# Sixty-four tokens return from the dense experts to the gathered ones, and sixteen expert products stand beside the gate table

## The chip, the core and the metric

One core of a Trainium2 chip runs the whole program. Its engines work side by side, each in the order in which its instructions stand: PE (TensorE, matrix products), DVE (VectorE), ACT (ScalarE), POOL (GpSimd, which here also issues the indirect gathers) and SP (SyncE, which issues the plain DMAs). Sixteen DMA engines move the data of both kinds of DMA. The metric is the device time of one execution in microseconds, the median of several runs.

## The reference

One layer of a hybrid decoder for a prompt of 1024 tokens and a sample group of 32 tokens (8 sequences of 4). The last part of it is where the time goes: each token picks 8 x 16 of 16384 experts by a product-key search, and sums their outputs.

```python
proj = x @ W_in                      # [z | x_ssd | B | C | dt | q | k | v]
m    = [SSD(...) ; DilatedWindowAttention(q, k, v)] @ W_out
h    = LayerNorm1(ALPHA * x + m)
# PEER(h), per token: 8 heads, 16 experts of 16384 each
s1, s2 = q[..., :128] @ keys_1, q[..., 128:] @ keys_2      # 128 keys each
e, g   = the 16 best of the pairs of the 16 best keys, softmax of their scores
hid    = gelu(u_tab[e] . h)
out    = LayerNorm2(ALPHA * h + sum((g * hid) * v_tab[e]))
```

All arrays are float32. The kernel splits an operand into a high and a low part and adds three products (high x high, low x high, high x low), so that a 1024-deep product of 128 outputs takes 24 matrix instructions for each piece of columns.

## The kernel before

**Two ways to the same expert sum.** Of the prompt tokens some are gathered: for each of its 128 picks a token fetches the expert's row of `u` (4 KB), DVE multiplies and sums it (L1871), and after the gelu it fetches the row of `v` and DVE adds it in (L1876). One instruction fetches one pick for 128 tokens, a `row` of 512 KB (L1845, on POOL's queue). The other tokens are dense: every expert is computed for every one of them, in 128 products with `ut` (128 experts each, "hidden") and 128 with `vd` (128 outputs each over 8 x 128 experts, "output"), and a table of gates that is zero nearly everywhere weighs the hidden values. The table is built on the chip (`gates`), stored to DRAM (`gd`) and read back chunk by chunk.

**Stages.** Part 0 handles the first 512 prompt tokens and the 32 sample tokens, part 1 the other 512 prompt tokens. Each part runs `first` (projections and attention), `second` (convolutions, the scan over chunks, and z), `third` (output projection and norm) and `route` (the key search). `dense` then does the expert products for TE tokens in two pieces of columns, `TPC`. Before, EXTRA = 64 prompt tokens of part 0 are taken out of the gathered group and put beside part 1's 512 and the 32 samples: TE = 608 in pieces of 320 and 288 columns, and 448 gathered tokens. These make 3 full groups of 128 tokens (256 rows each), and one of 64, whose 128 picks are packed as two halves of 64 partitions (`half_e`, `half_g`) and so take 128 rows: 896 rows.

**What sets the order.** The program is written out by hand. A product (`step`, `proj`, `product`) hands its instructions to PE in a number of equal shares, and after each share a tick runs every waiting generator ("lane") by its rate. `GATHER` sets how many rows the gather lane (`gathers`, `pumping`) takes for each projection of part 1: 2.5 in `first`, 3.2 in `second`, 3 in `third`, none in `route`, and 0.2 for each tick beside the table. In `dense` the rate spreads what is left evenly over the ticks. `LOOK` = 5 rows are fetched ahead into `ROWS` = 6 buffers, so the fetch of row k+5 waits until DVE has used row k-1.

**The table and what stands beside it.** `gates` takes four tokens at a time (a group): DVE compares (L1624, `oo`), POOL multiplies (L1626), PE multiplies four times (L1633), ACT copies out (L1643). 608 tokens make 152 groups. The list `EARLY` gives the ticks of the expert products that run between the groups: six of the first chunk's eight hidden products, in 8 to 40 shares. The last two of that chunk follow when the table is done.

**The dense loop.** For each chunk c of 1024 experts there are eight hidden products (PE writes PSUM, ACT gelu L1689, DVE weighs L1693, ACT and DVE split into `ah`, `al`), then eight output products that DVE adds up (L1717). Each product's 512 KB of weights is loaded in two halves (`wraw`), split by ACT (`whi`, L366) and by DVE or POOL (`wlo`, L367, by the list LO5 one in seven on DVE), two products ahead of its use. During a chunk's output products the next chunk's table is read (`g<-gd`). L447 and L1767 are the matrix instructions; in the first pass over the weights, part 0, split weights are stored to DRAM (`ws`), and part 1 loads these.

## Time and profile before

| | |
|---|---|
| median of 3 runs | 3749.65 us (3748.82 to 3754.33) |
| the profiled execution | 3745.24 us |
| span of its instructions | 3743.3 us |
| PE / DVE / ACT / POOL busy | 3461.4 / 2600.5 / 1205.4 / 2231.0 us |
| moved by DMA | 994.91 MB, of it 469.82 MB by POOL's queue |
| mean granted clock of PE | 0.965 of full speed |

The span runs from the first to the last instruction of the core, so the execution is 1.9 us longer than it. Busy shares are means over stages with different limits; what follows reads stages one at a time. A DMA share is the mean busy share of the 16 DMA engines in a stretch, and it can read a few hundredths above 1.

### The profile page before, as it was taken

The page shows a single profiled execution, that of the slowest core. Times are in us where ns is not written, and L with a number is a line of the kernel's source. Part 1 is how long each engine was busy: PE and PEld are TensorE (multiplying, and loading weights), DVE is VectorE, ACT ScalarE, POOL GpSimd, SP SyncE. Part 2 cuts the span into 40 slices and gives each one's busy share as a digit, 9 for nine tenths or more (in the row PEclk, how much of TensorE's full clock was granted, in tenths as well). Part 3 has the DMA queues.
Part 4 walks back from the last instruction along what each step waited for, and adds up shares of the span by engine and source line. Part 5 has one row for each costly group of instructions (what it writes and reads, how often), then busy time and mean ns, then how long its engine had stood idle before and what let it go on. Part 6 is the DMA issues. An engine that isn't in the chain of part 4 may idle for free.

```text
span 3743.3 us, 61910 instructions
## 1 busy us (share of the span) xinstructions
PE 3461.4 (92%) x22691; PEld 3132.8 (84%) x22691; DVE 2600.5 (69%) x5394; ACT 1205.4 (32%) x2195; POOL 2231.0 (60%) x2138
## 2 busy tenths in 40 slices
PE   7999999989799888896778999999999999999998
PEld 6757778988567666675777999999999999999997
DVE  2325654379668987589998867677767667777775
ACT  3422224252343233123565222222232222223223
POOL 3303555333444676313887877777778777777774
PEclk9999899999899999997889999999999999999999
DMA  7565447996557669742557999999999999999994
GB/s 248 192 207 185 144 149 241 371 343 214 163 168 293 235 217 337 304 141 72 202 204 267 342 328 339 336 322 314 320 326 356 330 329 335 321 315 321 333 330 138
DMA packets 452624, 994.91 MB, mean 266 GB/s; under 512 B 47712, under 2 KB 158688, under 8 KB 449376
## 3 DMA queue, kind: packets, MB, share of 16 engines
q1 hardware_dynamic: 323296, 521.14, 41.1%
q0 software_dynamic: 129024, 469.82, 34.6%
q8 instruction: 179, 2.93, 0.3%
q14 instruction: 125, 1.02, 0.1%
HBM read 845.18 MB, written 174.34 MB: 272 GB/s over the span
## 4 chain that ended last, share of the span: by engine, by line
PE 53%; DVE 16%; DMA 5%; POOL 5%; issue 4%; ACT 2%; SPq 0%; POOLq 0%; DVEq 0%; ACTq 0%
PE P L447 42%; PE P L1767 5%; DVE oo L1624 2%; DMA wlo<-ws 2%; DVE cv L751 2%; DVE row L1871 1%; PE P L712 1%; POOL row L1845 1%; DVE mr L1363 1%; PE P L689 1%; POOL oo L1626 1%; DVE keys L1367 1%; DVE keys L1361 1%; PE P L1633 1%; POOL eq L1564 1%
## 5 line engine op out<-in xcount | busy, mean ns | idle before, releaser
L367 POOL TENSOR_TENSOR wlo<-wraw,whi 128x512 fp32r<-128x512 f32 x524 | 678.5, 1300 | 495.6 <-ACT whi L366 438.5
L366 ACT ACTIVATE whi<-wraw 128x512 fp32r<-128x512 f32 (+1 forms) x668 | 406.1, 625 | 1305.7 <-PE P L447 563.7
L447 PE MATMUL P<-hh,whi 128*128 128x320 f32 (+3 forms) x2648 | 656.2, 313 | 13.4 <-DMA whi<-ws 5.7
L447 PE MATMUL P<-hl,whi 128*128 128x320 f32 (+3 forms) x2648 | 653.4, 311 | 3.2 <-POOL hl L1318 2.9
L447 PE MATMUL P<-hh,wlo 128*128 128x320 f32 (+3 forms) x2648 | 647.4, 310 | 7.6 <-DMA wlo<-ws 3.9
L1876 DVE SCALAR_TENSOR_TENSOR P<-row,hid,P 128x1024 f32<-128x1024 f32 x448 | 575.8, 1285 | 40.3 <-DMA row<-in_v,ecol 23.9
L1871 DVE SCALAR_TENSOR_TENSOR row<-row,P 128x1024 f32<-128x1024 f32 x403 | 478.8, 1214 | 66.1 <-DMA row<-in_u,ecol 29.6
L1845 POOL DMA_INDIRECT row<-in_u,ecol x384 | 386.9, 1008 | 191.6 <-DVE row L1871 100.9
L447 PEld LDWEIGHTS P<-hh,whi 128*128 128x128 f32 x2648 | 445.5, 191 | 24.9 <-DMA whi<-ws 7.0
L447 PEld LDWEIGHTS P<-hh,wlo 128*128 128x128 f32 x2648 | 443.7, 190 | 17.7 <-DMA wlo<-ws 5.9
L447 PE MATMUL P<-xh,whi 128*128 128x272 f32 (+4 forms) x1288 | 431.2, 345 | 27.0 <-ACT xh L366 15.0
L447 PEld LDWEIGHTS P<-hl,whi 128*128 128x128 f32 x2648 | 444.9, 191 | 12.6 <-POOL hl L1318 4.2
L1845 POOL DMA_INDIRECT row<-in_v,ecol x384 | 375.9, 979 | 118.4 <-DVE P L1876 47.1
L447 PE MATMUL P<-xl,whi 128*128 128x272 f32 (+4 forms) x1288 | 418.8, 335 | 7.4 <-POOL xl L367 6.8
L447 PE MATMUL P<-xh,wlo 128*128 128x272 f32 (+4 forms) x1288 | 417.4, 334 | 3.2 <-DMA wlo<-ws 3.2
L447 PE MATMUL P<-ah,wlo 128*128 128x320 f32 (+1 forms) x1536 | 341.8, 302 | 3.6 <-POOL wlo L367 3.6
L447 PE MATMUL P<-ah,whi 128*128 128x320 f32 (+1 forms) x1536 | 342.8, 302 | 0.0
L447 PE MATMUL P<-al,whi 128*128 128x320 f32 (+1 forms) x1536 | 341.5, 301 | 0.0
L447 PEld LDWEIGHTS P<-xh,whi 128*128 128x128 f32 (+1 forms) x1288 | 246.6, 195 | 57.5 <-ACT xh L366 16.6
L367 DVE TENSOR_TENSOR wlo<-wraw,whi 128x512 fp32r<-128x512 f32 (+1 forms) x144 | 133.6, 928 | 229.8 <-ACT whi L366 210.4
L447 PEld LDWEIGHTS P<-xl,whi 128*128 128x128 f32 (+1 forms) x1288 | 246.5, 195 | 33.9 <-POOL xl L367 8.7
L447 PEld LDWEIGHTS P<-xh,wlo 128*128 128x128 f32 (+1 forms) x1288 | 245.8, 195 | 29.4 <-DMA wlo<-ws 5.0
(386 smaller groups left out, 6110.7 us busy)
## 6 DMA issues: line engine op xcount, KB each, us to landing
wraw<-in_ut SPq DMA_DIRECT2D x256, 256.0 KB, 5.4
wraw<-in_vd SPq DMA_DIRECT2D x256, 256.0 KB, 5.0
ws<-whi SPq DMA_DIRECT2D x152, 256.0 KB, 5.1
ws<-wlo SPq DMA_DIRECT2D x152, 256.0 KB, 5.0
whi<-ws SPq DMA_DIRECT2D x152, 256.0 KB, 5.2
wlo<-ws SPq DMA_DIRECT2D x152, 256.0 KB, 5.5
gd<-gst SPq DMA_DIRECT2D x19, 2048.0 KB, 7.5
g<-gd SPq DMA_DIRECT2D x90, 320.0 KB, 10.9
```

The costliest lines, as they stand in the source:

```text
L366: nc.scalar.activation(hi, src, AF.Copy)
L367: (eng or nc.vector).tensor_tensor(lo, src, hi.bitcast(F32), op=ALU.subtract)
L447: nc.tensor.matmul(outs[i], w[a][:, k, :m], x[b][k][:, s:s + n], start=first and st, stop=last and sp)
L689: nc.tensor.matmul(sc[:, a:b], qz[:, hh, qt * 128:(qt + 1) * 128], kk[:, a:b], start=True, stop=True)
L712: nc.tensor.matmul(pv[row, :128], vv[:, k, row], pT[:, k, :], start=k == 0, stop=k == nt - 1)
L751: nc.vector.scalar_tensor_tensor(cv[:, 3:n], xr[:, k:k + m], cw[:, k:k + 1], cv[:, 3:n], op0=ALU.mult, op1=ALU.add)
L1361: nc.vector.max_index(idx[:, 0:8], vals[:, 0:8], src)
L1624: nc.vector.tensor_tensor(oo, iota.unsqueeze(1).unsqueeze(1).to_broadcast([128, 2, 4, 128]), eT[:, 0:2, t0:t0 + 4].unsqueeze(3).to_broadca ...
L1767: nc.tensor.matmul(outs[i][j], self.ws[q0 + i][wi][:, e, :], x[xi][e][:, s:s + m], start=e == p == 0, stop=e == last and p == 2)
L1845: nc.gpsimd.indirect_dma_start(out=rows[k], out_offset=None, in_=t["uv"[tab]], in_offset=bass.IndirectOffsetOnAxis(ap=tables(gi)[0][:, s:s ...
L1871: nc.vector.scalar_tensor_tensor(r, r, 1.0, at, op0=ALU.mult, op1=ALU.mult, accum_out=hid[:, s:s + 1])
L1876: nc.vector.scalar_tensor_tensor(at, r, hid[:, s:s + 1], at, op0=ALU.mult, op1=ALU.add)
```

## The change

The gathered group takes back the 64 tokens: 512 gathered tokens, 1024 rows, and TE = 544 dense tokens in pieces of 288 and 256 columns. The half-packed tables and their sum at the end go. The table has 136 groups. Beside it stand sixteen hidden products instead of six (`BEFORE`, `EARLY`): the eight of chunk 0, and the first two of each of chunks 1 to 4. The results of these last eight wait in DRAM (`ed`) until their chunk's turn, when `recall` loads them and `recalled` weighs and splits them. The dense loop (`STEPS`) has 240 products instead of 248. The rows of the gathers are drawn faster in part 1. The sample tokens' groups come first in the table, and its lane waits there until the key search is done.

```diff
-EXTRA = 64
-TG = TD - EXTRA
-NX = EXTRA + NS
-TE = PD + NX
+TE = PD + NS
...
-GATHER = [2.5, 3.2, 3, 0.0, 0.2]
+GATHER, GATHERT = [[0, 0, 0, 0], [4, 4.2, 3.5, 0.0]], 0.2
...
-EQ, OBUFS, EARLY = 4, 4, [8, 16, 24, 30, 34, 40]
+EQ, OBUFS, EARLY = 4, 4, [8] + [9] * 13 + [4] * 2
+AHEAD = {1: 2, 2: 2, 3: 2, 4: 2}
+BEFORE = [(0, 0, k) for k in range(8)] + [(c, 0, k) for c in AHEAD for k in range(AHEAD[c])]
+STEPS = [s for s in ((c, half, k) for c in range(NE // 8) for half in range(2) for k in range(8)) if s not in BEFORE]
...
+        self.ed = {(c, k): dpool.tile([128, TE], F32, name=f"ed{c}{k}") for c in AHEAD for k in range(AHEAD[c])}
...
-        work = [(NS, PD + EXTRA, 0), (EXTRA, PD, 128 - EXTRA)] + [(m, s, 0) for s, m in tiles]
-        given = 2
+        work = [(NS, PD)] + list((m, s) for s, m in tiles)
+        given = 1
...
-            if t0 == work[w][2] + work[w][0] - 4 * OBUFS:
+            if t0 == work[w][0] - 4 * OBUFS:
+                while w < given and self.top.live:
+                    yield
...
-        def early(k, ps):
-            gelu(r[:, k], ps)
+        def early(c, k, ps):
+            if c:
+                row = sp.tile([128, n], F32, name="er", tag="er", bufs=2)
+                gelu(row, ps)
+                nc.sync.dma_start(self.ed[c, k], row)
+            else:
+                gelu(r[:, k], ps)
+        def recall(c, k):
+            if k < AHEAD.get(c, 0):
+                waits[c, k] = dp.tile([128, n], F32, name="er", tag="er", bufs=2)
+                nc.sync.dma_start(waits[c, k], self.ed[c, k])
+        def recalled(c):
+            for k in range(AHEAD[c]):
+                row = waits.pop((c, k))
+                weigh(c, k, row)
+                yield
+                low(k, row, nc.vector)
+                yield
...
-        self.pumping.rate = self.left / ((len(steps) - 8) * DTICKS - 20)
-        for q, (c, half, k) in enumerate(steps[8:-LASTS], 8):
+        self.pumping.rate = self.left / (len(STEPS) * DTICKS - 20)
+        for q, (c, half, k) in enumerate(STEPS[:-LASTS], 1):
             if half:
                 table(c + 1, k // 4, k % 4)
+                recall(c + 1, k)
+            elif k == AHEAD.get(c):
+                self.fins.append(Lane(recalled(c), 1))
```

How the order of instructions moves, in three places. The names: `oo` is a group of the table, `hh` and `hl` are the dense tokens' split inputs, `cv` and `bc` the convolutions, `row` a gathered row, `r<-r,P` the sum of outputs; `al` closes a hidden product.

On PE beside the table, before:

```order
L1633 MATMUL P<-oo 128x128 x4
L447 MATMUL P<-hh,whi 128x320
L1633 MATMUL P<-oo 128x128 x4
L447 MATMUL P<-hh,whi 128x288
L1633 MATMUL P<-oo 128x128 x4
L447 MATMUL P<-hl,whi 128x320
```

and after:

```order
L1640 MATMUL P<-oo 128x128 x4
L450 MATMUL P<-hl,whi 128x288
L450 MATMUL P<-hl,whi 128x256
L450 MATMUL P<-hh,wlo 128x288
L450 MATMUL P<-hh,wlo 128x256
L450 MATMUL P<-hh,whi 128x288
L450 MATMUL P<-hh,whi 128x256
L1640 MATMUL P<-oo 128x128 x4
```

Where one or two pieces of an expert product stood between two groups, five or six stand now.

On DVE in `second` of part 1, at the convolutions, before:

```order
L751 SCALAR_TENSOR_TENSOR cv<-xr,convw,cv 128x512 x3
L1871 SCALAR_TENSOR_TENSOR row,hid<-row,gh 128x1024
L756 SCALAR_TENSOR_TENSOR bc<-xr,cv 128x512
L1871 SCALAR_TENSOR_TENSOR row,hid<-row,gh 128x1024
L751 SCALAR_TENSOR_TENSOR cv<-xr,convw,cv 128x512 x3
L1871 SCALAR_TENSOR_TENSOR row,hid<-row,gh 128x1024
L756 SCALAR_TENSOR_TENSOR bc<-xr,cv 128x512
L1871 SCALAR_TENSOR_TENSOR row,hid<-row,gh 128x1024 x2
```

and after:

```order
L754 SCALAR_TENSOR_TENSOR cv<-xr,convw,cv 128x512 x3
L1892 SCALAR_TENSOR_TENSOR row,hid<-row,gh 128x1024 x2
L759 SCALAR_TENSOR_TENSOR bc<-xr,cv 128x512
L1892 SCALAR_TENSOR_TENSOR row,hid<-row,gh 128x1024 x2
L754 SCALAR_TENSOR_TENSOR cv<-xr,convw,cv 128x512 x3
L1892 SCALAR_TENSOR_TENSOR row,hid<-row,gh 128x1024 x2
L759 SCALAR_TENSOR_TENSOR bc<-xr,cv 128x512
L1892 SCALAR_TENSOR_TENSOR row,hid<-row,gh 128x1024 x2
```

Between the convolutions one or two rows stood; now it is two each time. Over `second` DVE uses 105 rows instead of 80, over `first` 72 instead of 45, over `third` 49 instead of 42, and beside the table 33 instead of 34.

On DVE in the dense loop, from a late hidden product into the output products, before:

```order
L1876 SCALAR_TENSOR_TENSOR P<-row,hid,P 128x1024 x2
L1693 TENSOR_TENSOR P<-P,g 128x608
L1876 SCALAR_TENSOR_TENSOR P<-row,hid,P 128x1024
L1699 TENSOR_TENSOR al<-P,ah 128x608
L1876 SCALAR_TENSOR_TENSOR P<-row,hid,P 128x1024 x4
L1717 TENSOR_TENSOR r<-r,P 128x608
```

and after:

```order
L1897 SCALAR_TENSOR_TENSOR P<-row,hid,P 128x1024 x3
L1701 TENSOR_TENSOR P<-P,g 128x544
L1707 TENSOR_TENSOR al<-P,ah 128x544
L1897 SCALAR_TENSOR_TENSOR P<-row,hid,P 128x1024 x5
L1743 TENSOR_TENSOR r<-r,P 128x544
```

The tiles are narrower and the rows no fewer: 765 rows fall on the 238 products up to the last two (51.4 for 16 products), where 695 fell on 246 (45.2). After the table's last group PE has 3.2 products left beside the dense loop's 240, where it had 2.25 beside 248.

## Rows read from the trace of the kernel before

**Rows 1.** The page: busy time of two engines; in 40 slices PE, PE's clock, DMA.
```profile
PE 3461.4 (92%) x22691; PEld 3132.8 (84%) x22691; DVE 2600.5 (69%) x5394; ACT 1205.4 (32%) x2195; POOL 2231.0 (60%) x2138
...
PE   7999999989799888896778999999999999999998
...
PEclk9999899999899999997889999999999999999999
DMA  7565447996557669742557999999999999999994
```

**Rows 2.** The chain that ended last, 2040 to 3660 us: share by line.
```profile
by line: PE P L447 82.6%; PE P L1767 11.8%; DMA wraw<-in_ut 1.2%; issue 1.2%; DMA lng<-in_ln 1.0%; POOL wlo L367 0.5%; DVE r L1693 0.4%; POOL row L1845 0.3%; POOL acc L1901 0.2%; DVE al L1699 0.2%; ACT whi L366 0.1%; SPq L406 0.1%; ACT L168
```

**Rows 3.** PE in order of time: start us, busy us, instruction; two widths.
```profile
1546.99 0.40 PE L447 MATMUL P<-xh,whi 128*128 128x256 f32 x2
1547.23 0.40 PE L447 MATMUL P<-xl,whi 128*128 128x256 f32 x2
...
2500.03 0.44 PE L447 MATMUL P<-ah,wlo 128*128 128x320 f32 x2
2500.31 0.44 PE L447 MATMUL P<-ah,whi 128*128 128x320 f32 x2
```

**Rows 4.** One chunk's output and next hidden products: busy us by engine, clock, DMA share, GB/s.
```profile
2798.60:2852.20 53.60, 53.60 (x387) 53.60 (x386) 40.17 (x61) 12.30 (x20) 43.72 (x41) 1.00 1.01 367
2852.20:2905.90 53.70, 53.70 (x386) 53.70 (x385) 40.24 (x65) 18.02 (x31) 43.22 (x41) 1.00 0.97 344
```

**Rows 5.** The same two stretches, the gathers alone: POOL busy (count), clock, DMA.
```profile
2798.60:2852.20 53.60, 24.58 (x26) 1.00 1.01 367
2852.20:2905.90 53.70, 23.50 (x25) 1.00 0.97 344
```

**Rows 6.** Stretches with the highest DMA shares; columns as in rows 4.
```profile
2195.00:2215.00 20.00, 20.00 (x146) 20.00 (x145) 15.90 (x25) 3.17 (x5) 16.54 (x16) 1.00 1.05 386
2610.00:2630.00 20.00, 20.00 (x146) 20.00 (x145) 13.02 (x13) 3.68 (x6) 14.90 (x14) 1.00 1.05 384
1500.00:1550.00 50.00, 40.68 (x181) 30.95 (x180) 32.29 (x28) 0.00 (x0) 26.84 (x28) 0.93 1.04 400
```

**Rows 7.** Groups by line, 2500 to 3000 us: busy us, mean ns, idle before.
```profile
L1876 DVE SCALAR_TENSOR_TENSOR P<-row,hid,P 128x1024 f32<-128x1024 f32 x118 | 151.7, 1285 | 5.9 <-DMA row<-in_v,ecol 3.9
L1871 DVE SCALAR_TENSOR_TENSOR row<-row,P 128x1024 f32<-128x1024 f32 x95 | 113.2, 1215 | 22.3 <-DMA row<-in_u,ecol 17.1 <-issue 4.8
...
L367 POOL TENSOR_TENSOR wlo<-wraw,whi 128x512 fp32r<-128x512 f32 x128 | 165.6, 1298 | 59.9 <-ACT whi L366 52.2 <-issue 6.6
L1845 POOL DMA_INDIRECT row<-in_v,ecol x114 | 109.5, 960 | 32.5 <-issue 16.0 <-DVE P L1876 8.5 <-PE P L447 1.8
```

**Rows 8.** L1845, 2500 to 3000 us: its idle time without a cause, and landing.
```profile
  issue: 28.7, 107
...
DMA to landing us min/median/max: 4.5/6.5/10.4
```

**Rows 9.** Beside the table: the stretch (as rows 4), then groups (as rows 7).
```profile
1732.00:2018.00 286.00, 220.41 (x1500) 203.89 (x1501) 272.82 (x385) 172.01 (x176) 228.15 (x212) 0.88 0.54 199
...
L1624 DVE TENSOR_TENSOR oo<-P,eT 128x1024 f32<-128x1024 f32 x151 | 177.1, 1215 | 6.3 <-ACT eT L1587 2.8 <-PE P L1585 2.1 <-PE P L1633 1.3
...
L1564 POOL TENSOR_TENSOR eq<-eq,cf 128x1024 f32<-128x1024 f32 x8 | 18.9, 2367 | 0.0
...
L1633 PE MATMUL P<-oo x1216: 270/275/583, 1732.8 to 2017.7; 128*128 128x128 f32 x174
```

**Rows 10.** Part 1: `first` and `second` (as rows 4), chains of 1150 to 1340, 1430 to 1570 us.
```profile
1000.00:1050.00 50.00, 50.00 (x277) 37.54 (x276) 35.00 (x72) 20.32 (x50) 29.56 (x21) 1.00 0.58 181
1200.00:1250.00 50.00, 41.05 (x204) 31.48 (x203) 47.27 (x74) 15.75 (x31) 34.16 (x41) 0.93 0.89 329
...
by line: DVE cv L751 33.1%; DVE row L1871 26.0%; issue 6.3%; POOL row L1845 5.5%; DVE y L756 4.5%; ACT cv L749 2.5%; DVE y L955 2.5%; DVE E L950 2.3%; DVE xd L920 2.0%; DVE xe L921 2.0%; PE P L910 1.6%; DVE hst L952 1.5%; DVE E L951 1.5%; P
...
by line: DMA wlo<-ws 50.5%; PE P L447 19.5%; issue 10.9%; POOL row L1845 7.3%; POOL xl L367 3.0%; POOL ss L1152 2.5%; POOL y L1144 2.5%; POOL hl L367 1.3%; PE P L1162 0.8%; SPq L422 0.7%; PE P L1293 0.5%; DVE rsum L1216 0.3%; DVE r L1208 0.
```

More of the change, by code (lines that the diff above doesn't have):

```diff
@@ L350, in start @@
         self.close("xr")
+        self.smpp = self.open("smp", side="right")
         for dst, src in load:
@@ L398, in weights @@
                     self.kept[q] = names[key]
-        for c in range(NE // 8):
-            self.srcs += [t["ut"][c * 8 + k] for k in range(8)] + [t["vd"][c, k] for k in range(8)]
+        self.srcs += [t["vd"][c, k] if half else t["ut"][c * 8 + k] for c, half, k in BEFORE + STEPS]
     def load(self, q, i):
@@ L519, in part @@
         if self.smp:
-            xp = self.open("smp", side="right")
+            xp = self.smpp
             self.sconv = xp.tile([128, 20, NB, 3], F32, name="sconv")
@@ L544, in first @@
         if hf:
-            self.top.rate, self.pays = TOPS2, self.nc.vector
-        chooser = self.lane(self.chooses(), CHOOSE) if hf else None
+            self.top.rate, self.pays = TOPS2[hf], self.nc.vector
+            self.chooser = self.lane(self.chooses(*self.routed), CHOOSE)
         for w in ORDER[hf]:
             if w < 0:
-                if chooser:
-                    self.settle(chooser)
-                cp = self.open(f"cv{hf}", 2, side="right")
-                self.cp = cp
+                if self.last:
+                    self.settle(self.chooser)
+                self.cp = self.open(f"cv{hf}", 2, side="right")
+                cp = self.cp
                 self.bc = cp.tile([128, 8, self.T], F32, name="bc", bufs=1)
@@ L1155, in gated @@
             yield
-            while k < 11 and self.at < 3:
+            while k < 11 and self.at < TICKS[self.hf][1] - 1:
                 yield
@@ L1382, in route @@
         self.turns = LO4[hf]
-        self.routed = self.tiles[:n], self.best
+        self.routed = self.tiles[:n], self.best, self.sbest if self.smp else None
+        held = SCORES[hf]
         if self.last:
-            others = [self.lane(self.experts(sp, *v)) for v in zip(((self.smp_e, self.smp_g), (self.ecol[-1], self.gate[-1])), (NS, 128), self.given)]
+            others = [self.lane(self.experts(sp, (self.smp_e, self.smp_g), NS, self.given))]
         else:
-            self.gp = self.open("g")
+            if not hf:
+                self.gp = self.open("g")
             self.xrp = sp
@@ L1456, in pairs_room @@
         if self.last:
-            self.given = [pool.tile([128, 3, 128], F32, name=f"eT{i}") for i in range(2)]
+            self.given = pool.tile([128, 3, 128], F32, name="eT")
         return [pool.tile([128, n, PH, TK], d, name=f"best{i}") for i, d in enumerate((F32, U32, F32))]
@@ L1673, in dense @@
         hs = [[v[:, k] for k in range(8)] for v in self.h]
-        steps = [(c, half, k) for c in range(NE // 8) for half in range(2) for k in range(8)]
-        gs, ah, al = {}, {}, {}
+        gs, ah, al, waits = {}, {}, {}, {}
         self.turns = LO5
@@ L1812, in dense @@
         for i, (s, m) in enumerate(TPC):
[L1813 removed]
+            for j, (c, half, k) in enumerate(STEPS[-LASTS:]):
                 ps = self.P[:, PAIRS[j] + i, :m]
@@ L1850, in seat @@
             return dst
-        for k in range(LOOK):
-            fetch(k)
+        fetch(LOOK - 1)
         for k, (gi, tab, s) in enumerate(plan):
-            m = min(128, TG - gi * 128)
+            while ahead[0] <= k:
+                fetch(k)
+                yield
             hs = heads[gi]
```

167 lines of the change are left out of this document (78 added, 89 removed).

## The prediction

> **What bounds the kernel now.** I read the page's slices first, to split the run into stages, then the chain of waits of each stage, then tables of stretches. PE is busy 92% of the span, but unevenly: from slice 22 on (about 2040 us) its digit stays at 9 and its granted clock at full speed, while DMA stands at 9 too [rows 1]. This is the dense loop, and there the chain of waits is PE's own matrix instructions, 82.6% at L447 and 11.8% at L1767 [rows 2]. PE is the bound there, and nothing keeps it waiting for long: in a pair of stretches that hold one chunk's eight output products and the next chunk's eight hidden ones, PE is busy for all of 53.6 and 53.7 us [rows 4], which is 6.71 us a product. The reader is to see what else is in the same two lines: DMA has a share of 1.01 and 0.97, POOL is busy 43.7 us and DVE 40.2. PE wins this stage by a little. Between 1732.8 and 2017.7 us the table is built, and there DVE is busy 272.8 of 286 us while PE runs at 0.88 of its clock and waits in between [rows 9]. In part 1 the chain has two places: around 1150 to 1340 us it goes through DVE (convolutions 33%, rows 26%), and around 1430 to 1570 us half of it is the DMA that brings split weights back [rows 10].
>
> **The change, part by part.** All sums are against the profiled execution, 3745.24 us, which is 4.4 us below the median of the runs.
>
> *Dense loop, PE's side.* Two instructions of 256 columns start 0.24 us after the pair before, two of 320 and 288 columns 0.28 (0.279 over many pairs, 6.71 us / 24) [rows 3, 4]. Between these, 544 columns take 0.240 + 32/96 x 0.039 = 0.253, and a product of 24 such pairs 6.07 us. After the table's last group there are 243.2 products instead of 250.25. Before: 250.25 x 6.71 = 1679 us, and the other 46.6 us from 2017.7 to the end of the span are starts, the last norm and stores, which I leave as they are. On PE alone the stage would take 243.2 x 6.07 = 1476 us, 203 less.
>
> *Dense loop, the side of DMA.* The rows don't shrink with the columns: 51.4 of them for 16 products, and the stretches of rows 4 already carry 26 + 25 [rows 5]. They moved 367 x 53.6 + 344 x 53.7 = 38.1 MB in 107.3 us. The narrower table takes off 0.26 MB (64 of 608 columns of 2.49 MB a chunk). The 37.9 MB that are left should pass in 16 x 6.07 = 97.1 us, which is 390 GB/s. The engines' own time in the two stretches is 1.01 x 53.6 + 0.97 x 53.7 = 106.2 us, less 0.7% for the table 105.5. So at PE's pace DMA would need a share of 1.09, and no stretch shows that: 1.05 with 384 to 386 GB/s in 20 us, 1.04 with 400 GB/s in 50 us [rows 6]. DMA takes over from PE as the bound. At 1.05 and more a product takes 105.5/1.05/16 = 6.28 us, at 1.04 6.34, at 1.00 6.59. I take 6.34, since 1.04 is what the longest busy stretch of rows 6 holds. The 3.2 products in front of the loop have few rows beside them and go at 6.07. Sum: 3.2 x 6.07 + 240 x 6.34 = 1541, against 1679: -138 us. Ends: -203 (PE remains the bound) and 3.2 x 6.07 + 240 x 6.59 = 1601, so -78.
>
> Here a rule speaks against the change. The Trainium skill, "DMA: Bandwidth & Descriptors", Specifications, gives HBM about 358 GB/s for each core, half of what a stack delivers to two. By it a pair of halves needs 37.9 MB / 358 = 106 us, 6.6 us a product, and the stage gains 71 us instead of 138. The trace of this one-core run shows 400 GB/s for 50 us [rows 6], so the rule has no more than the chance of the second rival, which comes to nearly the same time by other means.
>
> *Dense loop, POOL and DVE.* POOL fetches a row in 0.96 us and then stands for about 0.2 us without a cause (28.7 us in 107 cases) [rows 7, 8], and of the 16 half weights of eight products it splits six in seven, 13.7, at 1.30 us each: 26 x 1.16 + 13.7 x 1.30 = 48 us of the 50.7 that eight products take at 6.34. It fits, at 95%. DVE: 26 rows x 1.29 = 33.5, and the rest of its 40.2 us (6.7) gets a tenth smaller: 39.5 of 50.7. Neither becomes the bound by itself, but PE is left with less slack behind both: the splits stand behind POOL's fetches, which wait for DVE's use of a row four rows earlier, and DVE's sums of outputs stand behind its rows. Splits run two products ahead of their use, some 12 us, and that is the cover that lets me charge nothing for these waits.
>
> *Products moved beside the table.* Ten more stand there (nearly 13 of the 16 lie between groups, the rest after). To DVE they add one in seven of their splits there; what weighs and splits their results runs in the dense loop as before. PE has the room: 13 x 6.07 = 79 us and the groups' small products in about 275 us. The sixteen groups that go free DVE of 16 x 1.215 = 19 us [rows 9]. Against this, the table's lane now waits after the sample tokens for the key search and then for the first tile's choice, which alternates DVE with two POOL multiplies of 2.4 us [rows 9] and used to have groups in between; I charge 8 us, and 1 for the extra splits. Sum: -10 us (0 to -20). If POOL's 20 extra splits of 1.28 us were not hidden by its idle 58 us, they would cost 26 and turn it to +16. The DRAM detour moves 8 x 0.28 MB out and back, 4.5 MB, some 12 us of DMA; out it lies in a stretch with a share of 0.54 [rows 9] and costs nothing, back it is about 6 us of a busy one, inside the range.
>
> *Rows in part 1.* `first` takes 27 more; DVE is busy 35 of 50 us and PE is the bound [rows 10], so they hide; I charge 3 us (27 x 1.29 = 35 without that cover). `second` takes 25 more, 25 x 1.29 = 32 us on DVE, which was busy 47 of 50 us and is the chain there [rows 10]; the last quarter of the stage is looser, so +24 (10 to 32). `third` takes 7 more of 0.52 MB where DMA is the chain at 400 GB/s [rows 6, 10]: +9. Sum: +36 (15 to 45).
>
> **Total:** -138 - 10 + 36 = -112 us, 3633 for the profiled execution, 3638 for the median.
>
> **The rivals.**
> *PE remains the bound* (6.07 a product). For it: the hidden half is at a share of 0.97 only [rows 4], and five rows in flight could fill its quiet spots with what the output half left over. Against it: 390 GB/s would be needed as a mean, which only the best 20 us reach. -203 - 10 + 36 = -177: 3573.
> *DMA at a share of 1.00* (6.59). For it: the best whole output stretch has 1.01 [rows 4], and every wait of DVE for a row leaves a gap in requests. -78 - 10 + 36 = -52: 3698.
> *Slower: five rows ahead are too few.* A row's cycle is its landing, DVE's use (1.29) and POOL's issue (1.16), with five in flight. With landing 6.5 us [rows 8] that is 8.95/5 = 1.79 us a row, and 3.21 rows a product make 5.75: no bound. But landing stretches as DMA fills up; at its largest, 10.4 us, the cycle gives 2.57 us a row and 8.25 us a product, some 350 us slower. The point: the total is zero at (1679 - 19 - 26)/240 = 6.81 us a product, that is 2.12 us a row, a median landing of 8.2 us. Against it: most of the landing would then be queueing behind the same five rows, which DMA's rate already counts. If it decides by a little (landing 8.5), a product takes 7.03 and the run 3803.
> *The change doesn't do what it says:* the ten moved products lengthen the table by their whole 61 us, because each group waits behind five matrix instructions on PE and POOL's splits. -138 + 51 + 36 = -51: 3699.
>
> **How the numbers follow.** Chances: forecast 0.51 (3600 to 3675), PE bound 0.17, share 1.00 0.18, products not hidden 0.05, slower 0.09. The range reaches from near the first rival, with part 1 at its cheap end, 3555, to the second with part 1 at its dear end and the table at 0, 3717. What one measurement of this kernel can tell from no change is about 0.2%, 7.5 us. Faster 0.89, same 0.02, slower 0.09.
>
> **What would show it right or wrong.** Right: in the dense loop PE waits in output halves, where the table is read, and less or not in hidden halves; the DMA share stands at 1.02 to 1.05 with 370 to 385 GB/s; DVE's idle time in front of its row instructions is put down to DMA; a pair of halves takes 101 us. PE's granted clock should stay at full speed, 2.4 GHz, as it does now [rows 4]; in rows 6 it reads 0.93 in a stretch where PE is busy 40.7 of 50 us, so a lower one would show long gaps; a pair of 105 us or more with shares below 1.00 speaks for the second rival or for the cycle of five, and then the median landing (8 us and more) tells them apart. The table's stretch should be 270 to 280 us and `second` some 24 us longer than before. It is wrong altogether if PE stands busy throughout, or if DVE rather than DMA is what PE waits for.

## The result, and the profile after

| | kernel before | changed kernel |
|---|---|---|
| median | 3750.84 us (3748.82 to 3754.33, 4 runs) | 3718.22 us (3715.19 to 3721.76, 4 runs) |
| profiled span | 3743.3 us | 3713.3 us |
| first group of the table's products | 1732.8 us [rows 9] | 1794.5 us |
| last group of the table's products | 2017.7 us [rows 9] | 2068.8 us |
| from there to the end of the span | 1725.6 us | 1644.5 us |

The ratio is 0.9922, with a 95% interval of 0.9907 to 0.9937. The changed kernel is faster, by 0.8%. I had forecast 3638 us, a gain of 112; the gain is 32, and the time lies 1 us outside my range. In the two profiled executions the 30 us are: part 1 61.7 us longer (forecast 36), the table's stretch 10.6 us shorter (forecast 10), everything behind it 81 us shorter (forecast 138).

The lines of the page after that answer to [rows 1], the 40 slices of the span in tenths of busy time, with the queues' totals:

```profile
PE   7999999989798778779488799999899999899998
POOL 4303555333465667630488688888788887888885
PEclk9999999999899899889799899999999999999999
DMA  7665447996568867964156799999999999999995
GB/s 248 195 209 187 146 148 237 375 337 213 180 196 303 301 221 271 371 247 148 63 216 251 254 378 367 371 368 371 345 381 376 370 366 354 351 373 368 375 375 189
...
q1 hardware_dynamic: 316896, 516.88, 40.6%
q0 software_dynamic: 147456, 536.94, 38.8%
```

Counted from 0, from slice 23 on DMA stands at 9 and moves 345 to 381 GB/s in each slice but the last; PE has slices of 8 now. The last slice, and the two in front of slice 23, are not at that rate. That matters below.

The dense loop in stretches, as in [rows 4]: the first eight output products, an output and a hidden half in the middle, the last output half, then the middle of the loop and all of it (columns: length, busy us and count of PE, weight loads, DVE, ACT, POOL; PE's granted clock, DMA share, GB/s).

```profile
2111.40:2165.30 53.90, 52.54 (x386) 51.05 (x387) 48.21 (x68) 12.94 (x21) 41.45 (x36) 0.95 0.81 284
...
2697.90:2748.10 50.20, 48.87 (x388) 48.65 (x387) 39.83 (x65) 11.30 (x20) 41.05 (x39) 1.00 1.03 384
2747.90:2796.90 49.00, 48.58 (x388) 48.36 (x387) 40.92 (x70) 17.18 (x30) 42.87 (x41) 1.00 1.01 378
...
3633.00:3683.40 50.40, 45.63 (x344) 44.84 (x342) 29.32 (x35) 12.16 (x20) 37.59 (x30) 0.97 0.60 220
...
2150.00:3600.00 1450.00, 1376.88 (x10634) 1364.42 (x10632) 1167.01 (x1509) 397.17 (x676) 1195.48 (x1103) 0.97 1.00 368
...
2111.40:3691.50 1580.10, 1499.11 (x11531) 1483.83 (x11532) 1266.75 (x1626) 435.03 (x739) 1291.96 (x1183) 0.97 0.98 358
```

The same middle stretch of the kernel before, which has PE busy for all but 6 us of it:

```profile
2150.00:3600.00 1450.00, 1443.68 (x10314) 1442.97 (x10313) 1039.06 (x1336) 397.11 (x661) 1082.76 (x988) 1.00 0.94 329
```

So PE is no longer the bound. A quiet pair of halves takes 99 us (2697.9 to 2796.9), which is even less than the 101 that I forecast; the loop as a whole takes 1580 us for 240 products, 6.58 us each, against 6.34.

What PE and DVE waited for in the changed kernel from 2125 to 3660 us (total us, times, longest):

```profile
PE P L450 <- DVE r L1743: 28.9, 17, 5.8
PE P L450 <- DVE al L1707: 23.3, 13, 3.7
PE P L450 <- POOL wlo L371: 16.9, 7, 10.1
...
DVE row L1892 <- DMA row<-in_u,ecol: 109.6, 117, 3.4
DVE P L1897 <- DMA row<-in_v,ecol: 94.0, 107, 3.4
```

PE's waits name DVE and POOL, as if those were too slow. The two lines of DVE tell what is behind: it waits 204 us for gathered rows, and the sums and splits that PE needs stand behind those rows in DVE's order. My prediction had called it wrong altogether if DVE rather than DMA is what PE waits for, so which of the two readings holds is what the experiments had to settle.

### The profile page after: what moved, and what is told of

The parts are those of the page before. It is cut to its first block, busy times and chain, and to the rows that moved or that the text cites. A ratio compares the mean times of both kernels' runs of the same rounds, so it can differ in the third digit from the quotient of the medians.

```text
span 3713.3 us, 62101 instructions
## 1 busy us (share of the span) xinstructions
PE 3310.6 (89%) x22560; PEld 2972.8 (80%) x22560; DVE 2711.9 (73%) x5565; ACT 1176.9 (32%) x2178; POOL 2336.3 (63%) x2250
## 3 DMA queue, kind: packets, MB, share of 16 engines
q0 software_dynamic: 147456, 536.94, 38.8%
## 5 line engine op out<-in xcount | busy, mean ns | idle before, releaser
L1897 DVE SCALAR_TENSOR_TENSOR P<-row,hid,P 128x1024 f32<-128x1024 f32 x512 | 657.9, 1285 | 130.5 <-DMA row<-in_v,ecol 120.9
L450 PE MATMUL P<-hh,whi 128*128 128x288 f32 (+3 forms) x2648 | 632.4, 304 | 44.2 <-DVE al L1707 23.3
L1866 POOL DMA_INDIRECT row<-in_u,ecol x512 | 517.9, 1012 | 218.0 <-DVE row L1892 88.9
L450 PE MATMUL P<-hh,wlo 128*128 128x288 f32 (+3 forms) x2648 | 625.2, 301 | 10.7 <-POOL wlo L371 5.8
L450 PE MATMUL P<-hl,whi 128*128 128x288 f32 (+3 forms) x2648 | 626.8, 302 | 2.8 <-POOL hl L1322 2.5
L1892 DVE SCALAR_TENSOR_TENSOR row<-row,P 128x1024 f32<-128x1024 f32 x440 | 526.9, 1215 | 137.3 <-DMA row<-in_u,ecol 112.7
L1866 POOL DMA_INDIRECT row<-in_v,ecol x512 | 496.4, 970 | 173.4 <-issue 69.9
L450 PE MATMUL P<-ah,whi 128*128 128x288 f32 (+1 forms) x1536 | 328.0, 293 | 25.2 <-DVE r L1743 25.1
L450 PE MATMUL P<-ah,wlo 128*128 128x288 f32 (+1 forms) x1536 | 326.5, 293 | 15.0 <-POOL wlo L371 15.0
L450 PE MATMUL P<-al,whi 128*128 128x288 f32 (+1 forms) x1536 | 325.1, 292 | 0.0
```

The lines of the kernel that those rows point to most:

```text
L450: nc.tensor.matmul(outs[i], w[a][:, k, :m], x[b][k][:, s:s + n], start=first and st, stop=last and sp)
L1866: nc.gpsimd.indirect_dma_start(out=rows[k0], out_offset=None, in_=t["uv"[tab]], in_offset=bass.IndirectOffsetOnAxis(ap=self.ecol[gi][:, s: ...
L1892: nc.vector.scalar_tensor_tensor(r, r, 1.0, at, op0=ALU.mult, op1=ALU.mult, accum_out=hid[:, s:s + 1])
L1897: nc.vector.scalar_tensor_tensor(at, r, hid[:, s:s + 1], at, op0=ALU.mult, op1=ALU.add)
```

## The experiments

The theories, by the letters that the expectations use: A, the loop stands at what DMA carries; B, the waits among POOL, DVE and PE hold it; C, too few rows are in flight; D, single holes in which PE and DMA run dry; F, only the rows' latency counts. G and H are about part 1. "Before" is the kernel before, run beside each group.

**1. The old row rates in part 1.**

```
-GATHER = [..., [4, 4.2, 3.5, 0.0]]
+GATHER = [..., [2.5, 3.2, 3, 0.0]]
```

> The changed kernel with one part undone: in part 1 the rows come at the rates of the kernel before (2.5, 3.2 and 3 a step instead of 4, 4.2 and 3.5), so about 60 rows more are left for the dense loop. Both theories expect part 1 to be some 60 us shorter than in the changed kernel (the first group of the table at about 1733 instead of 1794.5 us). They differ on the dense loop. Theory A, the loop stands at what DMA carries, 360 to 375 GB/s: 60 rows of 0.52 MB are 31 MB, 84 us at 370 GB/s, so about 3740 us in all, 20 slower than the changed kernel. Theory B, the loop is held by waits between POOL, DVE and PE that don't grow with the bytes: the loop gets at most some 20 us longer, about 3675 in all.

Measured: 3747.19 us, 1.0001 of before (0.9984 to 1.0018). Part 1 gave its 63 us back (first table group at 1731.0), and the 59 rows cost the stretch behind the table 93 us (1622.4 to 1715.6 between the table's last group and the last output product). That is A's side, and a little more than its 84. It also shows where the change's whole gain sits: with narrower products and moved products but the old rates, nothing is gained. The changed kernel gathers four groups of 128 tokens where the kernel before had three and a half (1024 gathered rows in the trace against 896). At the 93/59 = 1.58 us that a row costs the loop here, 128 more rows are some 202 us, an estimate, and that is as much as the 203 us that the narrower products would have saved on PE alone.

**2. Half of DVE's work on the rows, the same bytes.**

```
-...scalar_tensor_tensor(at, r, hid[:, s:s + 1], at, ...)
+...scalar_tensor_tensor(at[:, :w], r[:, :w], hid[:, s:s + 1], at[:, :w], ...)   # w = 512 in the dense loop
```

> The changed kernel, but in the dense loop DVE uses only the first 512 of the 1024 columns of each fetched row (half of that part of the computation is left out); every row is still fetched whole. DVE's instruction falls from about 1.29 to 0.65 us, the bytes stay. Theory A (the loop stands at what DMA carries): a product stays at 6.5 to 6.6 us, the total within 15 us of the changed kernel's 3718. Theory B (rows come free too late because DVE holds them, so POOL issues late and DMA is starved): a product falls to 6.1 to 6.35 us, 3610 to 3665 in all, with the DMA share at 1.04 or above.

Measured: 3710.86 us, 0.9905 (0.9881 to 0.9929), 7 us below the changed kernel. Its middle stretch:

```profile
2150.00:3600.00 1450.00, 1374.92 (x10704) 1363.90 (x10702) 809.79 (x1516) 400.46 (x676) 1197.71 (x1109) 0.98 1.01 370
```

DVE is busy 810 instead of 1167 us and the loop hardly moves. Its waits from 2125 to 3660 us:

```profile
DVE row L1894 <- DMA row<-in_u,ecol: 247.4, 187, 11.5
DVE P L1899 <- DMA row<-in_v,ecol: 235.6, 192, 4.1
...
PE P L451 <- DVE r L1744: 26.5, 10, 6.9
```

DVE now waits 483 us for rows, where it waited 204, and PE still waits for DVE's sums as it did. What DVE was spared it spends waiting. So DVE's own time isn't the cause, and B falls for DVE.

**3. Half of the rows' bytes, the same work for DVE and POOL.** The table is addressed as rows of 512 columns, and DVE reads each twice.

```
-nc.gpsimd.indirect_dma_start(out=rows[k0], out_offset=None, in_=t["uv"[tab]], ...)
+tb = t["uv"[tab]]
+tb = tb if self.wide == D else tb.rearrange("e (a d) -> (e a) d", a=2)
+nc.gpsimd.indirect_dma_start(out=rows[k0][:, :self.wide], out_offset=None, in_=tb, ...)   # self.wide = 512 in the dense loop
```

> The changed kernel, but in the dense loop each fetch brings rows of 512 columns, half the bytes, and DVE reads those twice, so its instructions are as long as before (the result of that part is not the reference's). POOL issues as many fetches. Theory A (bytes): the rows' 26.8 MB of the 38 MB that 16 products move become 13.4, DMA no longer limits, and a product falls to PE's 6.07 to 6.15 us: 100 to 120 us off, about 3600 to 3620. Theory B (DVE's and POOL's time for a row): a product stays above 6.4 us, 3680 or more.

Measured: 3660.01 us, 0.9769 (0.9748 to 0.9791): 58 us less, where DVE's halved work gave 7. Bytes count, but A's 100 to 120 didn't come. A hidden half, an output half and the middle stretch of this run:

```profile
2925.00:2973.20 48.20, 48.20 (x387) 48.20 (x386) 41.69 (x43) 15.91 (x28) 41.95 (x40) 1.00 0.78 235
2973.10:3024.30 51.20, 49.01 (x388) 48.40 (x387) 42.63 (x41) 12.07 (x20) 44.35 (x43) 1.00 0.84 262
...
2150.00:3600.00 1450.00, 1409.51 (x11076) 1399.25 (x11075) 1220.46 (x1561) 415.21 (x709) 1254.16 (x1150) 0.99 0.80 247
```

The hidden half stands at PE's floor, 48.2 us or 6.03 a product. The output half doesn't, at a share of 0.84: there PE waits for POOL's splits (32 us in 18 cases from 2111 to 3660 us). POOL is busy 44 of 51 us. In the middle it is busy 1254 us and stands for another 155 without a cause, 97% of the 1450 together. So the next bound, some 60 us below the first, seems to be POOL; no run took its work away to show it. DVE still waits 165 us for rows in this run, at a share of 0.80: that wait comes with a full DMA and with late fetches alike, and only the total tells them apart.

**4. Two more rows in flight.**

```
+if self.more and k0 % 8 > 5: rows[k0] = self.more.tile(..., tag="rowx", bufs=2)
-fetch(k + LOOK)
+fetch(k + self.look)   # 5, from the dense loop on 7
```

> The changed kernel with eight row buffers and seven rows fetched ahead in the dense loop, instead of six and five. Theory A (DMA is full at a share of 0.98 to 1.01): only the queue in front of the engines gets longer, the median landing goes from 7.0 to about 9.5 us, a product stays at 6.5 to 6.6 us and the total within 8 us of 3718. Theory C (DMA runs dry between issues, and my 1.04 would come with more rows in flight): a product falls towards 6.34 us, 3660 to 3690 in all, share 1.03 or more.

Measured: 3714.38 us, 0.9918 (0.9901 to 0.9936), the same as the changed kernel. The waits from 2125 to 3660 us and the middle stretch:

```profile
PE P L451 <- POOL wlo L372: 48.5, 25, 12.1
...
DVE wlo L372 <- ACT whi L371: 103.8, 25, 14.0
...
DVE rowx L1897 <- DMA rowx<-in_u,ecol: 25.2, 13, 9.1
DVE row L1897 <- DMA row<-in_u,ecol: 23.2, 21, 3.1
...
DVE P L1902 <- DMA row<-in_v,ecol: 13.0, 16, 3.0
...
DVE P L1902 <- DMA rowx<-in_v,ecol: 9.7, 10, 2.0
...
2150.00:3600.00 1450.00, 1367.95 (x10652) 1353.75 (x10651) 1157.10 (x1514) 403.22 (x680) 1201.87 (x1107) 0.98 1.00 369
```

DVE's waits for rows shrink from 204 us to the 71 of these four lines, and in their place DVE waits 104 us for the high half of a weight (18 in the changed kernel), and PE waits for splits. The rows came earlier, the bytes and the total stayed. Why ACT's high half came later isn't shown: ACT's own waits for loads are no longer than in the changed kernel. C falls, and so does my "five rows ahead are too few". The changed kernel's own rows say the same: from 2500 to 3500 us they landed in 7.0 us in the median, where the prediction took 8 us and more as the sign of that rival.

**5. Two products of chunk 0 behind the table.**

```
+LATE = [(0, 0, 6), (0, 0, 7)]   # done after settle(table_lane) and the first table reads
```

> The changed kernel with the order of its sixteen early products altered: two of chunk 0 are done last, after the table's lane is finished and the first reads of the table are issued, so PE has 12 us of work while those reads, the weighting and the splits run. In the changed kernel PE stood still 17.5 us there and the eight products behind it ran at 6.74 us. Theory D (a stretch in which PE and DMA run dry is lost for good): 10 to 16 us off, 3702 to 3708. Theory A alone (only the mean rate of DMA counts, and idle time of PE is made up for later): within 4 us of 3718.

Measured: 3716.07 us, 0.9924 (0.9898 to 0.995). PE's wait in front of the first output product fell from 17.5 to 10.5 us, and the total stayed. That fits A, by which a gap of PE alone is made up as long as DMA is the bound; but with two runs, 6 us apart, and an interval of about 10 us to each side, a gain of the 7 us can't be excluded.

**6. More rows in the first stage of part 1, fewer in the others.**

```
-GATHER = [..., [4, 4.2, 3.5, 0.0]]
+GATHER = [..., [6, 3.2, 3, 0.0]]
```

> The changed kernel with the rows of part 1 moved: rates 6, 3.2, 3 instead of 4, 4.2, 3.5, so that only the first stage (attention) takes more rows than before, some 36 more than in the changed kernel, and the other two take as many as before the change. By the stage times (27 more rows in the first stage cost about 4 us, 25 in the second about 35, 7 in the third about 25) the two later stages give back 60 us; the total of rows for the dense loop stays nearly the same. If the 36 rows stay hidden (DVE was busy 36 of 50 us there): 3660 to 3675. If DVE becomes the bound of the first stage: 36 x 1.29 = 46 us more, 3700 to 3710.

Measured: 3717.76 us (3707.54 to 3726.07), 0.9936 (0.9912 to 0.9959): no gain. The rows were not hidden in `first`. Its attention ended 7 us later than in the changed kernel (1163 against 1156 us), and `second`, at its old rate, had its last convolution at 1386 us, against 1333 before and 1372 in the changed kernel.

**7. The norm of a finished token group taken apart.** Its weights are loaded once, and its steps go into a lane of their own.

```
+steps = self.norm2(acc, t["y"][gi * 128:gi * 128 + 128], 128)   # with a yield between its steps
+if self.lnw and gi < NTG - 1:
+    self.lane(steps, 0.5)
```

> The changed kernel with the norm of a finished group of 128 tokens taken apart in the dense loop: its weights are loaded once beforehand into tiles of their own, and its instructions are issued two steps of the order apart instead of in one block. In the changed kernel POOL stood 9.0 and 9.9 us in front of that block's multiply and fetched no row for 10 to 15 us, twice, and the product halves around it took 61.8 and 63.1 us instead of about 50. Theory D: both stretches fall to 51 to 55 us, 15 to 25 us off, 3693 to 3703. Theory A alone (DMA's mean rate sets the loop, the hole is made up for later): within 5 us of 3718.

In the changed kernel POOL at one such norm (start, length, idle time ahead and its releaser), and the two halves that hold one:

```profile
3140.71 1.30 POOL L371 TENSOR_TENSOR wlo<-wraw,whi 128x512 fp32r<-128x512 f32 x1
3151.91 4.76 POOL L1918 TENSOR_TENSOR acc<-acc,lng 128x1024 f32<-128x1024 f32 x2 [9.90 <-DVE row L1892]
3156.82 0.98 POOL L1866 DMA_INDIRECT row<-in_u,ecol  x1
...
2636.30:2698.10 61.80, 55.66 (x386) 55.25 (x387) 43.84 (x73) 17.57 (x30) 51.83 (x47) 0.87 0.89 325
...
3107.30:3170.40 63.10, 51.73 (x387) 51.10 (x386) 42.20 (x48) 14.79 (x23) 45.74 (x41) 0.89 0.91 327
```

For 15 us POOL issues no fetch. With the norm spread, the halves there read:

```profile
2647.50:2703.70 56.20, 51.94 (x384) 51.06 (x384) 48.05 (x74) 18.30 (x32) 48.05 (x43) 0.94 0.95 336
3165.60:3220.40 54.80, 49.75 (x386) 48.38 (x385) 42.26 (x70) 18.14 (x31) 48.64 (x44) 1.00 0.97 354
```

Measured: 3702.17 us (3698.28 to 3712.8), 0.9893 (0.9863 to 0.9923). The halves are shorter by 6 and 8 us and DMA's share in them is higher. The intervals of the two kernels' ratios overlap, so 16 us is the likely size, not a sure one; together with two other edits (run 16) the gain is clear. It is what one expects if a hole in DMA's own work is lost.

**8. No table reads after chunk 0.**

```
+if c:
+    gs[c, i] = gs[0, i]
```

> The changed kernel without the table's reads after chunk 0: the gates of chunk 0 are used for all chunks (so the result of that part isn't the reference's). 2.2 MB of about 38 MB a chunk go, in pieces of 512 bytes, 7 to 8% of the engines' busy time. Theory A (DMA's total work, whoever moves it, sets the loop): 60 to 110 us less, down to what PE and the two holes at the groups' norms allow, 3620 to 3660. Theory F (only the gathered rows matter, by their latency, and the other transfers are beside it): less than 20 us off.

Measured: 3661.3 us (one run), 57 us less. F falls: bytes of any kind count.

**9. One sixth of PE's work left out, all transfers kept.**

```
+ops = [op for op in ops if op[0] % 2 or op[1] == 0]   # in the dense loop
```

> The changed kernel, but in the dense loop four of each product's 24 pairs of matrix instructions are left out (the low half of the weights for every second part of the sum, so the result is a little less exact). PE's floor falls from 6.07 to 5.06 us a product; every transfer stays. Theory A (DMA's total work sets the loop at 365 to 366 GB/s, the rate of all runs so far that keep the bytes): a product stays at 6.45 to 6.6 us, 3695 to 3720. Theory D (PE's waits and the holes around them cost the time, and DMA could do more if PE asked): 6.0 to 6.25 us a product, held by POOL's 48 us for eight, 3570 to 3640.

Measured: 3732.03 us, 0.9952 (0.9935 to 0.9968), slower than the changed kernel. Its middle stretch:

```profile
2150.00:3600.00 1450.00, 1209.90 (x8736) 1171.78 (x8735) 1157.06 (x1502) 394.21 (x669) 1183.63 (x1090) 0.93 1.00 364
```

PE is busy 1210 of 1450 us, its granted clock is at 0.93 of 2.4 GHz on average, and DMA still stands at 1.00. The loop has nothing to gain from PE, and D as the main cause falls. The total lies 12 us above the range of A, so something beside the bytes made this run slower; what, stays open.

**10. The table in pieces of 1 KB.**

```
-gs[c, i] = dp.tile([128, n // 32, 4, 32], ..., bufs=2)
+gs[c] = dp.tile([128, n // 32, 8, 32], ..., bufs=1)
```

> The changed kernel with the gates' table read in pieces of 1 KB (eight experts) into one tile instead of 512 bytes (four experts) into two. The bytes stay; the packets of 512 bytes took 28 ns, those of 2 KB about 90, so 1 KB should take about 48 instead of 56 for two. Theory A1, what is full is the engines' busy time (share 1.00): 14% of the table's 7 to 8% of it, about 1%, 12 to 18 us less, 3700 to 3706. Theory A2, what is full is a rate of bytes (365 GB/s): within 5 us of 3718.

Measured: 3716.62 us, 0.9917 (0.9895 to 0.9939), no change.

**11. The old rate in the third stage alone.**

```
-GATHER = [..., [4, 4.2, 3.5, 0.0]]
+GATHER = [..., [4, 4.2, 3, 0.0]]
```

> The changed kernel with the rate of the third stage of part 1 alone put back (3 instead of 3.5, about 7 rows). By the stage times that stage became 25 us longer by the change, against 9 in the prediction, and only 5 us with the rate of 3 in the run with rows in the first stage only. If these seven rows are the cause: 15 to 20 us off in part 1, about 10 back in the dense loop, 3705 to 3712. If the stage is longer because DVE and POOL come late into it with rows of the stage before: within 5 us of 3718.

Measured: 3736.65 us (3733.06 to 3746.11), 0.9971 (0.996 to 0.9982), 18 us slower than the changed kernel, which nobody expected. Part 1 became only 4.9 us shorter (first table group at 1789.6), and the seven rows cost about 10 in the loop. The rest I can't explain: the loop ran at 365 GB/s instead of 368, but so did the changed kernel when it ran again (run 15, 3719 us), and the same rate in the next kernel did no harm. An edit of seven rows can move the total by 18 us without a cause that was found, so single differences of that size (runs 2, 5, 7 and 9) say little by themselves.

**12. Four edits together** (5, 7, 10 and 11).

> The changed kernel with four edits together: the spread norm, two products behind the table, the third stage's old rate, and the table in pieces of 1 KB. If DMA's work is the bound and the edits are independent, the sum of what they give alone: about -15 (norm), 0 to -3 (products), -5 to -10 (third stage), 0 to -15 (table), so 3675 to 3698, faster than both kernels. If they only shift the same idle time: 3695 to 3702, no better than the spread norm alone.

Measured: 3693.37 us, 0.9856 (0.9836 to 0.9877).

**13 and 14. Half of DVE's use, or half of the bytes, in part 1 only.** The edits are those of 2 and 3, up to the table.

> The changed kernel, but in part 1 DVE uses only the first 512 columns of each fetched row (half of that part of the computation is left out there); all rows are fetched whole, in the same places. Part 1 became 62 us longer with 59 more rows (first table group 1732.8 to 1794.5 us). Theory G, DVE's time is what the rows cost in part 1, in all three stages together: 231 rows lose 0.64 us each, 148 us of DVE work, and the first table group comes at 1710 to 1740 us, so that part 1 is no longer than in the kernel before. Theory H, the fetches' transfers or POOL's issues are the cost: the first table group stays at 1780 to 1795.

> The changed kernel, but in part 1 each fetch brings a row of 512 columns, and DVE uses it twice in two instructions, so that its time per row stays about 1.3 us (the result of that part isn't the reference's). 231 x 0.26 = 60 MB fewer pass in part 1. Theory G (DVE): the first table group comes at 1775 to 1795 us, only the last stage of part 1, where DMA stood at 400 GB/s, gains some 5 to 15. Theory H (transfers): 1735 to 1755.

Measured: 3693.99 us (0.982 to 0.9887 of before) and 3701.05 us (0.9841 to 0.9903). The table's groups in the changed kernel, with half the use and with half the bytes:

```profile
L1640 PE MATMUL P<-oo x1088: 270/275/583, 1794.5 to 2068.8; 128*128 128x128 f32 x182
```

```profile
L1641 PE MATMUL P<-oo x1088: 270/275/583, 1769.4 to 2045.3; 128*128 128x128 f32 x182
```

```profile
L1641 PE MATMUL P<-oo x1088: 270/275/583, 1769.4 to 2044.3; 128*128 128x128 f32 x182
```

Each gives back 25 us, neither 62, and they give it in different places:

| us | last convolution (`second`) | from there to the norm of `third` | first table group |
|---|---|---|---|
| before | 1333 | 234 | 1732.8 |
| changed | 1372 | 259 | 1794.5 |
| half the use | 1351 | 253 | 1769.4 |
| half the bytes | 1373 | 233 | 1769.4 |

In `third` its 25 us vanish with half of the bytes and not with half of the use, so bytes hold this stretch. That all 25 come from added bytes isn't shown, since run 14 fetches fewer bytes there than the kernel before did. In `second` half of the use takes off 21 of 39 us; as it halves the work of all the rows and not only of the added ones, DVE's part is at most that. Of the bytes in `second` run 14 says nothing: it reads each half row twice, and DVE's instructions for a `u` row took up to 1.85 us instead of 1.27 to 1.46, so that between 1156 and 1373 us the rows cost DVE 119 us instead of 103. The other 18 us stay open; POOL's issues (1.0 us each, and as many in both runs) are what neither run changed.

**15 and 16. The changed kernel once more, and three edits** (5, 7 and 10, with the rates of the changed kernel).

> The changed kernel itself once more, beside the others of this call, to compare with them on the same chip: 3712 to 3722 us by all theories.

> Three edits together: the spread norm, two products behind the table and the table in pieces of 1 KB, with the rates of the changed kernel (the run with four edits also had the third stage's old rate, which alone made the kernel about 18 us slower). If that rate costs 18 us here too: 3670 to 3680. If it was an accident of how the rows fell in that one kernel: 3688 to 3698, as with four edits. If the table and the products give nothing and only the norm counts: 3700.

Measured: 3719.15 us, 0.9917 (0.9895 to 0.9939), for the changed kernel, and 3693.13 us, 0.9845 (0.9827 to 0.9863), for the three edits. So the latter beat both kernels, by 0.7% and 1.5%, and the third stage's rate doesn't matter beside them. The spread norm is the only one of the three that showed anything alone.

**17 and 18. PE out of the way, and the table's pieces dropped or enlarged.**

> Two edits together: four of each product's 24 pairs of matrix instructions left out in the dense loop, and no reads of the table after chunk 0 (chunk 0's gates are used throughout). With the first edit alone the loop stood at 364 GB/s and a share of 1.00, 6.6 us a product. If DMA's ceiling is a rate of bytes near 368 GB/s, whatever the pieces: 36.3 MB for 16 products in 98.7 us, 6.17 us a product, 3625 to 3650 in all, share 0.95 or less. If the pieces of 512 bytes hold the rate down and rows and weights alone pass at some 390 to 400 GB/s, as in 50 us of part 1: 5.7 us, so that POOL's 6.0 us would bind, 3585 to 3610.

> Two edits together: the matrix instructions left out as in the run with less PE work alone (3732 us, 364 GB/s at a share of 1.00), and the table in pieces of 1 KB. PE no longer covers what the larger pieces save. If the engines' busy time is the ceiling: about 1% of the loop, 3712 to 3720. If it is a rate of bytes: within 6 us of 3732 with a share of 0.99.

Measured: 3666.97 us, 0.9778 (0.975 to 0.9806), and 3722.19 us, 0.9925 (0.9897 to 0.9954). The middle of the first of them:

```profile
2150.00:3600.00 1450.00, 1239.93 (x9131) 1202.87 (x9130) 1224.57 (x1552) 414.67 (x705) 1238.40 (x1142) 0.95 0.97 357
```

Without the small pieces DMA didn't go to 390 GB/s; it stood at 357 and a share of 0.97, with POOL busy 85%, and 95% with the 143 us in which it stands without a cause, so POOL may be what holds this run. The total is 6 us above run 8, which had all of PE's work, and outside both ranges. The 10 us that larger pieces gave beside less PE work lie inside the two intervals. Runs 10, 17 and 18 speak against the table's 512-byte pieces as the ceiling without settling it; whether it is a rate of bytes or something in the order of the fetches at this rate stays open.

## Why the prediction was wrong

**DMA becomes the bound: right in the main.** Runs 2, 4 and 9 shrink DVE's work, put more rows in flight and shrink PE's work; all three leave the loop at 364 to 370 GB/s and the total between 3711 and 3732. Only fewer bytes shorten it much (runs 3, 8 and 17, 51 to 58 us). DVE idle for rows was as I had said. Other signs were off: the share is 1.00 instead of 1.02 to 1.05, the rate 368 GB/s instead of 370 to 385, and PE's granted clock 0.97 in the middle instead of full speed. And PE's waits name DVE and POOL; runs 2 and 3 together put those of DVE down to the bytes. What they show is that the loop's time follows its bytes and not DVE's work, PE's work or the rows ahead; that DMA could carry no more isn't shown (see the last section).

**The bytes: right.** 358 GB/s over 1580.1 us is 565.7 MB, 37.7 MB for 16 products, against 37.9 forecast.

**"I take 6.34, since 1.04 is what the longest busy stretch of rows 6 holds": this is the step that failed.** It has two parts. 37.9 MB in 16 x 6.34 = 101.4 us is 374 GB/s. In the 1450 us of the middle DMA moved 368, norms included: 533.6 MB, which at 374 would have taken 1427, so 23 us. The other 130 us of the loop moved 32.1 MB, 86 us' worth at 374: 44 us lost. They are the first output half (share 0.81, behind PE's 17.5 us wait for the table) and the last one (share 0.60, where rows and weights run out). Together 67, less 8 for the slightly smaller bytes, and 59 is what the loop took more: 1580 against 240 x 6.34 = 1522. I had priced all 240 products at a peak, and at a steady one. A peak of 50 us from another stage is no mean over 1450 us, and a stage that DMA bounds loses what DMA does not carry at its ends. In the kernel before PE was busy 101.5 of 103.1 us in two such stretches (2037.9 to 2090.0 and 3625.0 to 3676.0 us), at shares of 0.85 and 0.88. This account goes by bytes. Counted in products, the middle took 221.5 at 6.55 us each and lost 46 us to 6.34, and the other 18.7 took 6.96 and lost 12; the ends moved fewer bytes for a product. Either way the term that failed is the share of 1.04 as a mean: it was 1.00 in the middle and 0.98 over the loop. The end at 0.60 I didn't try to fill; filling a part of the front gap (run 5) gave nothing that can be measured.

The rival with a share of 1.00 put the loop at 6.59 a product and the run at 3698. The loop went that way, to 6.58, so I had the case but gave it 0.18. The Trainium skill, "DMA: Bandwidth & Descriptors", Specifications, gives about 358 GB/s for a core from HBM, and the mean over the loop is 358 GB/s. By an estimate from that figure the stage gains 71 us in my sum; it gained 81. I had set it aside for the 400 GB/s of 50 us [rows 6]. The trace agrees with the figure as a mean over the loop, in part by chance, since the ends with their low shares are in it, and not as a limit, since the middle moves 368 and quiet halves move 378 to 384 GB/s.

**The table, -10 with ten more products hidden: right.** Its stretch went from 285 to 274.3 us, 10.6 less. DVE's busy time there fell by about 22 us, where the forecast had 19 less 1 for splits, and its idle time grew by some 11, where it had 8 of waiting; what the single terms cost was not measured. The rival in which the products aren't hidden is out.

**Part 1, +36: wrong, it was +61.7.** `first` at +3 came out near (its attention ends 5 us later), but "so they hide" did not hold: when it ended, 27 of its 72 rows still stood in front of DVE, against 17 of 45 before. DVE takes them in order, so `second` starts behind with them, and run 6, with 109 rows in `first`, had its last convolution later still. `second` cost +35 instead of +24, and DVE was at most some half of it (run 13). `third`, forecast +9 for seven rows, cost +25, in a stretch that bytes hold (run 14). There I counted the seven rows that the rate adds. Putting that rate back (run 11) gave only 5 us, so the seven are not the cause; that later rows of `second` run there is my reading, not shown. PE's granted clock fell with it, from 0.96 before to 0.90 after as a mean of 1150 to 1400 us, where PE stands still more; how much of the 18 open us that is was not measured.

**Why the total still gained.** By run 1 the change's three parts are worth: narrower products, ten moved ones and 128 more rows to gather, together nothing; 59 rows moved out of a loop that pays 1.58 us for each (93/59) into a part that pays 1.05 (61.7/59), 30 us.

## What to carry to other kernels

When the edit takes work from the engine that is busy all the time, look for the second bound's mean over the whole stage, edges included, and price the stage with that, not with the best stretch that the trace shows anywhere. A wait that names an engine is settled by shrinking that engine's work and, in another run, the bytes behind it: here, by runs 2 and 3 together, what PE waited for at DVE was bytes. With DMA as the bound, less work or a shorter gap for PE gave nothing that could be measured (runs 5 and 9), while spreading out what stops the engine that issues the fetches probably gave 16 us (run 7), and 25 with two other edits (run 16).

## What was not expected of the hardware

- 16 DMA engines at a share of 0.97 to 1.01 carry 357 to 371 GB/s over 1450 us in every variant with full rows, though the same core carries 400 to 401 GB/s for 50 us in `third`, before and after. A share near 1 isn't a full load here, since packets that take long count as busy. In the middle of the loop a packet of 4 KB took 160 ns in the median, and 7% of such packets' time went into those of over one and a half medians; in the 50 us of `third` that was 0.2 to 0.4%. With the packet times of `third` the same packets would fill some 1345 of the 1450 us, an estimate. What lengthens them stays open; runs 10, 17 and 18 speak against the table's small pieces.
- Half rows travel in pairs. In run 3 POOL's queue counts 98816 packets against 147456, so in the loop two half rows of 2 KB went in one packet of 4 KB. The middle moved 247 GB/s there at a share of 0.80, against 368 at 1.00; the share isn't proportional to the rate, so one can't be worked out from the other.
- Less work for PE brought its clock down. With a sixth of it left out the granted clock was 0.93 in the middle of the loop, between the levels of 1.2 and 2.4 GHz, and PE was still busy 83% of the time. The first eight output products behind the 17.5 us gap had 0.95 and took 6.74 us each.
